# Depthwise convolution of k and v as diagonal products on TensorE, with a re-costed plan, in a hybrid S5 / RWKV-7 layer

## Chip, cores and metric

One core of one Trainium2 chip. The metric is device time of one launch in microseconds (us); less is better.

## What is computed

One layer over 512 latent tokens x (an 8 x 64 grid, 1024 channels) with 256 context tokens in front, all in float32. mod_x and mod_c are nine vectors of 1024 from silu(c) @ w_mod + b_mod.

```python
x   = half_ffn(x, mod_x, 0, ...)
ctx = half_ffn(ctx, mod_c, 0, ...)
hc, hx = modulate(ctx, ...), modulate(x, ...)
_, ctx_states = token_mixers(hc, 1, zero_states, p, False)
out_x, _ = token_mixers(hx, rows, ctx_states, p, True)
x = x + mod_x[5] * out_x
x = half_ffn(x, mod_x, 2, ...)
return rmsnorm(x, final_g)
```

token_mixers projects with w_in into u, r|k|v, three low-rank pieces and two gates; u runs through a bidirectional S5 (a complex recurrence of 64 states in each of 32 groups); r, k and v go through a depthwise 3x3 convolution (`centred_conv`, zero padding; one row of 256 for the context) and then a bidirectional RWKV-7 with 8 heads of 64. Both results are normed, gated, projected and summed.

## The kernel before

**Data.** Activations lie with channels on partitions and tokens along the free axis. A float32 product is made as three fp32r products (`mm3`: hi x hi, lo x hi, hi x lo): each 128 x 1024 weight item is loaded raw by SP, ACT casts it to wh, and POOL or DVE subtracts to give wl (`w_split`, L306, which picks the engine of the subtraction). One item of w_in for the latent tokens is then 24 products of 128 x 512 on PE.

**Order.** The work is written as generators with priorities. A planner (`Plan`, L52) keeps a modelled time for every engine, and at build time runs the generator of best priority whose needs are ready by its model; so it writes one fixed program, and each engine then works through its own rows strictly in order. All DMAs are issued by SP, also in order. A DMA into a buffer that is still read holds up every DMA behind it on SP.

**Stages.** (1) Modulation, then the context's first FFN. (2) The latent tokens' first FFN, with the context's mixers as side streams. (3) b1 (`phase_b1`, `win_items` L1126, `win_mm` L1154): latent projections in the order low-rank pieces, four u items, then k, v, r for each j = 0..3 (a j is 128 channels, two heads); for each a convolution, then `pa`, `pn` and `pb` (L1267 to L1419), which scale k by decays into the RWKV operands (tiles nb, kt, st) and send them to DRAM (abk, lf). `s5_in` (L1690) multiplies u (tiles U, gt), and `s5_rec` (L1723) runs 63 dependent steps of four 128 x 64 operations on POOL (tiles t, hs). `fill_run` (L542) is 16 modulation units of j = 5..8, each two 512 KB loads (wmod, two buffers), eight small products, a row copy (mrow) and two products with sel. (4) b2 (`phase_b2`, L1793): the RWKV chunks (tiles AB, M, Z, Tl), `s5_out` (L1741: tiles hs, gt, U, Tz), `s5_post` (gelu, tiles yi, ga, yg), the glu items, with the 17 gate items of w_in as filler on PE. (5) The output projections. (6) The second FFN of the latent tokens.

**The convolution.** `conv_evac` copies the projection from PSUM into a padded tile (10 x 66, on ACT), makes the centre tap on ACT, and `conv` adds eight taps on DVE, per block of 128 channels:

```python
V.scalar_tensor_tensor(o3, pad[:, dy:dy + 8, dx:dx + 64], cw[:, t:t + 1], o3,
                       op0=OP.mult, op1=OP.add)
```

There are 12 blocks (r, k, v for four j). Two pads alternate, so a block's evacuation waits for the convolution two blocks earlier.

**The products of pb.** Per j and direction d, nb, kt and two of the five st pieces are made on POOL, the other three on DVE:

```python
Pg.tensor_mul(nb, fw(nkk, d), ic)
Pg.tensor_mul(kt, kt, fw(k, d))
Pg.tensor_mul(st[hi, :, 1], nb[hi], em[hi, :, 1:65])
Pg.tensor_mul(st[lo, :, 1], kt[lo], em[lo, :, 1:65])
```

Every instruction is recorded under one line, so the trace is read by the names of tiles.

Of the kernel before, what the change touches and what calls it, by code (L numbers as in the profile page):

```python
# [28 lines left out]
SPD = 0  # L29
# [6 lines left out]
FILLP = 10  # L36
# [7 lines left out]
UAT = 0  # L44
# [7 lines left out]
class Plan:  # L52
# [8 lines left out]
    def __init__(self, nc):  # L61
        self.nc = nc
        self.free = dict.fromkeys("VAPTSHD", 0.0)
        self.w, self.r, self.ev, self.streams = {}, {}, {}, []
        self.tick, self.work, self.cold = 0, 0.0, False
        self.filler, self.quota, self.recent = None, None, []
        for name, e in (("vector", "V"), ("scalar", "A"), ("gpsimd", "P"), ("tensor", "T"), ("sync", "S")):
            setattr(self, name, PlanEngine(self, getattr(nc, name), e))
# [33 lines left out]
    def step(self, e, cost, out, ins, work=0.0):  # L102
# [3 lines left out]
        t = max(t, self.unread(out))  # L106
        if e == "T":
# [4 lines left out]
            self.work += work  # L112
# [75 lines left out]
class PlanEngine:  # L188
# [3 lines left out]
    def __getattr__(self, name):  # L192
        f, plan, e = getattr(self.eng, name), self.plan, self.e

        def g(out, *args, **kw):
# [4 lines left out]
            elif e == "T":  # L200
                k, m = min(i.partition_size() for i in ins), out.partition_size()
                n = out.nbytes() // (4 * m)
                if ins[0].dtype == F32R:
                    c = max(107.0, n / 2.4)
                elif name == "transpose":
                    c = n / 1.2
                else:
                    c = max(n, m) / 1.2 if min(m, k) <= 64 else max(n, 128) / 0.6
                    if m <= 32 and n > 128:
                        c = n / 2.4  # L210
                plan.step(e, c, out, ins, n * k * m / 16384 * (1 if ins[0].dtype == F32R else 2))
            else:
# [6 lines left out]
                elif e == "V" and name == "scalar_tensor_tensor":  # L219
                    a = 130  # L220
                elif e == "V" and name in ("tensor_scalar", "tensor_copy", "memset"):
                    b = 0.52
# [4 lines left out]
                plan.step(e, a + b * n, out, ins)  # L227
# [34 lines left out]
class Kern:  # L262
# [43 lines left out]
    def w_split(self):  # L306
# [16 lines left out]
        eng = nc.vector if (i < self.n_post + 2 or i >= self.n_ffn) and f["P"] - max(f["V"], self.sch.t) > SPD else nc.gpsimd  # L323
# [830 lines left out]
    def win_mm(self, r, m, wh, wl):  # L1154
# [6 lines left out]
        if M_R <= m < M_WD:  # L1161
            n, q = r.n_conv, len(r.names)
            r.n_conv += 1
            yield [f"conv{r.s}{n - 2}"] * (n >= 2) + [f"pb{r.s}{n // q - 2}", f"vr{r.s}{n // q - 2}"] * (n >= 2 * q)
# [3 lines left out]
        else:  # L1168
            self.win_evac(r, m, px)

# [34 lines left out]
    def conv_evac(self, r, n, m, px):  # L1205
# [3 lines left out]
        pad = r.pads[n % 2]  # L1209
        o = r.q.tile([128, r.n], F32, name="cv" + "rkv"[ch // 4], bufs=2)  # L1210
        if r.v:
            A_.copy(pad[:, 1:257], px)
        else:
            A_.copy(pad[:, 1:9, 1:65], px.rearrange("p (y x) -> p y x", x=64))
# [3 lines left out]

    def conv(self, r):
        V = self.nc.vector  # L1220
        for i in range(4 * len(r.names)):
            yield [f"cve{r.s}{i}"]
            n, ch, o = r.cvq[i]
            j, name = ch % 4, "rkv"[ch // 4]
            pad = r.pads[n % 2]
            cw = self.cw[:, ch]
            yield [pad, o, ("V", 500)]
            if r.v:
                for t in (0, 2):
                    V.scalar_tensor_tensor(o, pad[:, t:t + 256], cw[:, 3 + t:4 + t], o, op0=OP.mult, op1=OP.add)  # L1230
            else:
                o3 = o.rearrange("p (y x) -> p y x", x=64)
                for t in (0, 1, 2, 3, 5, 6, 7, 8):
                    dy, dx = divmod(t, 3)
                    V.scalar_tensor_tensor(o3, pad[:, dy:dy + 8, dx:dx + 64], cw[:, t:t + 1], o3,
                                           op0=OP.mult, op1=OP.add)
                    if t in (1, 3, 6):
                        yield [("V", 500)]
            r.cv[name, j] = o
            self.sch.post(f"conv{r.s}{n}")  # L1240
            self.sch.post(f"cv{name}{r.s}{j}")
# [25 lines left out]
    def pa(self, r):  # L1267
# [3 lines left out]
        for j in range(4):  # L1271
# [24 lines left out]
            for i in (2 * j, 2 * j + 1):  # L1296
# [3 lines left out]
                cm = q.tile([128, nch, 65], F32, name="cm")  # L1300
                V.tensor_sub(cm, s65, s65[:, :, 32:33].to_broadcast([128, nch, 65]))
                yield [cm, ("A", 1000)]
                ep = q.tile([128, nch, 65], F32, name="ep", bufs=2)
# [811 lines left out]
```

## Time and profile before

| | us |
|---|---|
| median of 3 runs | 1918.43 (1918.2, 1918.43, 1923.06) |
| the profiled execution | 1924.01, span 1922.3 |
| busy in the span: PE, DVE, ACT, POOL | 1701.1, 917.5, 721.4, 866.6 |
| mean granted clock of TensorE | 0.927 |

The stages, read from the trace, end at about 290 (context FFN), 890 (latent FFN), 1148 (b1), 1411 (b2), 1545 (output projections) and 1922 us (second FFN). The granted clock is a share of the upper of two levels, 2.4 GHz; the lower is 1.2 GHz. An fp32 product is recorded as two instructions.

### The profile page before, as it was taken

Reading aid. Unit: us, or ns where it says so; the run is one execution under the profiler, and the core shown is the slowest. Engines: PE = TensorE matmul, PEld = TensorE weight load, DVE = VectorE, ACT = ScalarE, POOL = GpSimd, SP = SyncE. Lnnn points to the kernel's source line nnn. Section 1 sums busy time; section 2 is a strip of 40 time slices with the busy share of each in tenths; the row PEclk is TensorE's granted clock in tenths of the full one; section 3 lists DMA queues with packets and bytes.
Section 4 is the critical chain, followed back from the end, with each engine's and each line's share of the span. In section 5 each row is a group of like instructions: output and inputs, shape, how many; then the busy total and the mean of one; then the engine's idle time right before and its main releaser. Section 6 shows DMA issues by size and latency. Waiting matters only on the chain.

```text
span 1922.3 us, 33127 instructions
## 1 busy us (share of the span) xinstructions
PE 1701.1 (88%) x13208; PEld 1411.5 (73%) x13208; DVE 917.5 (48%) x1680; ACT 721.4 (38%) x1205; POOL 866.6 (45%) x882
## 2 busy tenths in 40 slices
PE   6999998899999799988887458999987999999996
PEld 3789987677777667877665226777777988888886
DVE  3376454676757364136887616463433331111214
ACT  3355442345453134235554111356443342222221
POOL 1145442456556247432658984101165324444441
PEclk9989999898999899988998558999998999999998
DMA  9865541444554753343553566746364123233331
GB/s 309 299 193 186 189 143 56 123 125 126 148 164 128 199 177 98 91 150 99 164 173 115 158 202 196 217 134 182 128 198 152 56 77 99 89 98 99 101 108 44
DMA packets 235626, 278.43 MB, mean 145 GB/s; under 512 B 93616, under 2 KB 186800, under 8 KB 234448
## 3 DMA queue, kind: packets, MB, share of 16 engines
q1 hardware_dynamic: 235472, 276.32, 47.0%
q8 instruction: 104, 1.70, 0.4%
q14 instruction: 50, 0.41, 0.1%
HBM read 234.31 MB, written 43.22 MB: 144 GB/s over the span
## 4 chain that ended last, share of the span: by engine, by line
PE 55%; DVE 13%; DMA 11%; POOL 8%; ACT 6%; issue 6%; SPq 2%; DVEq 0%; ACTq 0%; POOLq 0%
PE b L196 55%; DMA wmod<-in_wmod 3%; POOL t L196 3%; SPq L196 2%; POOL wl L196 2%; ACT wh L196 2%; DMA AB<-abk 2%; DMA gt<-gates 1%; DVE wl L196 1%; DMA raw<-in_win 1%; DMA raw<-in_wgu 1%; DVE prod L196 1%; POOL hs L196 1%; DVE cvk L196 1%; DVE st L196 1%
## 5 line engine op out<-in xcount | busy, mean ns | idle before, releaser
L196 POOL TENSOR_TENSOR wl<-raw,wh 128x1024 fp32r<-128x1024 f32 x202 | 488.1, 2421 | 842.5 <-ACT wh L196 809.0
L196 PE MATMUL b<-hx,wh 128*128 128x512 f32 (+1 forms) x2432 | 704.4, 377 | 17.2 <-ACT wh L196 11.0
L196 PEld LDWEIGHTS b<-hx,wh 128*128 128x128 f32 x2432 | 441.0, 196 | 93.4 <-ACT wh L196 12.6
L196 PE MATMUL b<-hx,wl 128*128 128x512 f32 (+1 forms) x1216 | 451.2, 371 | 11.3 <-POOL wl L196 11.2
L196 ACT CAST wh<-raw 128x1024 fp32r<-128x1024 f32 x273 | 283.2, 1046 | 226.6 <-DMA raw<-in_wgu 102.7
L196 PEld LDWEIGHTS b<-hx,wl 128*128 128x128 f32 x1216 | 237.6, 195 | 53.4 <-POOL wl L196 14.9
L196 PE MATMUL b<-ah,wh 128*128 128x512 f32 (+1 forms) x560 | 200.4, 358 | 8.7 <-DVE prod L196 3.2
L196 PE MATMUL b<-al,wh 128*128 128x512 f32 (+1 forms) x560 | 196.7, 351 | 0.1
L196 PE MATMUL b<-ah,wl 128*128 128x512 f32 (+1 forms) x560 | 196.5, 351 | 0.1
L196 PE MATMUL b<-hc,wh 128*128 128x256 f32 x928 | 177.0, 292 | 1.2 <-ACT hc L196 1.2
L196 DVE TENSOR_TENSOR prod<-sil,b 128x512 f32<-128x512 f32 (+1 forms) x68 | 39.6, 583 | 262.8 <-PE b L196 245.3
L196 DVE TENSOR_TENSOR wl<-raw,wh 128x1024 fp32r<-128x1024 f32 x71 | 103.8, 1463 | 126.9 <-ACT wh L196 126.0
L196 PEld LDWEIGHTS b<-hc,wh 128*128 128x128 f32 x928 | 149.5, 197 | 10.5 <-issue 7.3
L196 PE MATMUL b<-hc,wl 128*128 128x256 f32 x464 | 133.3, 287 | 0.5 <-POOL wl L196 0.5
L196 PEld LDWEIGHTS b<-ah,wh 128*128 128x128 f32 x560 | 109.2, 195 | 25.3 <-DVE prod L196 3.8
L196 ACT CAST ah<-prod 128x512 fp32r<-128x512 f32 (+1 forms) x68 | 36.6, 538 | 233.6 <-DVE prod L196 233.6
L196 PEld LDWEIGHTS b<-ah,wl 128*128 128x128 f32 x560 | 109.2, 195 | 14.0 <-POOL wl L196 0.6
L196 PEld LDWEIGHTS b<-al,wh 128*128 128x128 f32 x560 | 109.5, 195 | 12.3 <-DVE al L196 0.3
L196 PE MATMUL b<-wmod,zs 128*32 128x256 f32 x576 | 62.5, 534 | 41.8 <-DMA wmod<-in_wmod 41.7
L196 DVE SCALAR_TENSOR_TENSOR x1c<-b,gp,x1c 128x512 f32<-128x512 f32 (+1 forms) x67 | 44.0, 662 | 100.2 <-PE b L196 100.2
L196 PEld LDWEIGHTS b<-hc,wl 128*128 128x128 f32 x464 | 91.2, 197 | 0.7 <-POOL wl L196 0.7
L196 ACT ACTIVATE sil<-b 128x512 f32<-128x512 f32 (+1 forms) x68 | 35.0, 515 | 144.1 <-PE b L196 143.9
(289 smaller groups left out, 2359.3 us busy)
## 6 DMA issues: line engine op xcount, KB each, us to landing
raw<-in_wgu SPq DMA_DIRECT2D x132, 512.0 KB, 3.6
wmod<-in_wmod SPq DMA_DIRECT2D x72, 512.0 KB, 6.0
raw<-in_wdn SPq DMA_DIRECT2D x66, 512.0 KB, 3.8
raw<-in_win SPq DMA_DIRECT2D x49, 512.0 KB, 4.1
gt<-GTd SPq DMA_DIRECT2D x32, 256.0 KB, 3.6
abk<-st SPq DMA_DIRECT2D x8, 1024.0 KB, 5.5
AB<-abk SPq DMA_DIRECT2D x8, 1024.0 KB, 6.3
Hd<-H SPq DMA_DIRECT2D x32, 128.0 KB, 1.9
```

The source lines that it names most:

```text
L196: r = f(out, *args, **kw)
```

## The change

- **Convolution.** For the latent tokens k and v (8 of 12 blocks) go to PE: `taps` (POOL) builds nine diagonal 128 x 128 matrices dg of one block, and `conv_mm` adds nine fp32 products of the unpadded 8 x 64 tile in one PSUM bank, each trimmed by `reach` to the tokens that its tap reaches (1 of 512 columns, 2 of 448, 2 of 504, 4 of 441). ACT copies the sum out. r (4 blocks) stays on DVE, trimmed in the same way. There are three pads.
- **pb.** nb, kt and the two st pieces go from POOL to DVE, for both kinds of token. `pa` does without the tile cm.
- **wl.** The subtraction goes to DVE unless POOL would be done sooner by the model (1150 ns there, 2300 ns on POOL), in the same ranges of items as before.
- **Order.** The u items stand behind k, v, r of j = 3 (UAT 3). The modulation filler has priority 5 and starts with b1. The planner's costs are replaced, and DVE and POOL share a port in its model.

In instructions: PE +72 products; DVE -96 convolution steps of 128 x 512, +32 trimmed steps and 4 scalings, +64 products of pb, wl 71 to 144; POOL wl 202 to 129, -64 products of pb, +8 builds of dg.

```diff
-FILLP = 10
+FILLP = 5
-UAT = 0
+UAT = 3
...
-                self.cold = self.work < 2800
+                self.cold = self.work < 1400
...
-                    c = max(107.0, n / 2.4)
+                    c = max(107.0, n / 2.4) + 13
...
+                port = e == "P" or e == "V" and sum(x.space != PSUM and x.free_size() > 1 for x in ins) > 1
+                plan.step(e, a + b * n, out, ins, port=port)
...
-        eng = nc.vector if (i < self.n_post + 2 or i >= self.n_ffn) and f["P"] - max(f["V"], self.sch.t) > SPD else nc.gpsimd
+        late = max(f["P"], self.sch.t) + 2300 > max(f["V"], self.sch.t) + 1150
+        eng = nc.vector if (i < self.n_post + 2 or i >= self.n_ffn) and late else nc.gpsimd
...
     def fill_run(self, pool):
+        yield ["qx"]
         yield from self.mod_run([(j, u) for j in (5, 6, 7, 8) for u in range(4)], pool, 2, lambda j: 2)
...
+    def taps(self, r, ch):
+        self.dg = r.q.tile([128, 9, 128], F32, name="dg")
+        self.nc.gpsimd.affine_select(self.dg, self.cw[:, ch, :, None].to_broadcast([128, 9, 128]),
+                                     pattern=[[0, 9], [1, 128]], base=0, channel_multiplier=-1,
+                                     compare_op=OP.is_equal, fill=0.0)
...
+    def conv_mm(self, r):
...
+        for i, t in enumerate((4, 0, 1, 2, 3, 5, 6, 7, 8)):
+            o, i_ = self.reach(t)
+            self.nc.tensor.matmul(o3[o], dg[:, t], pad[i_], start=i == 0, stop=i == 8, skip_group_check=True)
+            if i % 2:
+                yield
+        if ch < 11:
+            self.taps(r, ch + 4 if ch < 8 else ch - 3)
+        o = r.q.tile([128, r.n], F32, name="cv" + name, bufs=2)
+        self.nc.scalar.copy(o, px)
...
+            for t in (0, 1, 2, 3, 5, 6, 7, 8):
+                a, b = self.reach(t)
+                V.scalar_tensor_tensor(o3[a], pad[b], cw[:, t:t + 1], o3[a], op0=OP.mult, op1=OP.add)
...
-                Pg.tensor_mul(nb, fw(nkk, d), ic)
-                Pg.tensor_mul(kt, kt, fw(k, d))
+                V.tensor_mul(nb, fw(nkk, d), ic)
...
-                Pg.tensor_mul(st[hi, :, 1], nb[hi], em[hi, :, 1:65])
+                V.tensor_mul(st[hi, :, 1], nb[hi], em[hi, :, 1:65])
...
+                V.tensor_mul(kt, kt, fw(k, d))
```

Three places show how the rows move; (hx, wh or wl) is a projection item, (wmod, zs) a modulation unit.

PE, the end of b1, before: the last product of the last projection item, and what stands behind it.

```order
L196 MATMUL b_10617<-hx_109,wl 128x512
L196 MATMUL b_10519<-wmod,zs 32x256 x4
L196 MATMUL b_10669<-st 32x32 x32
L196 MATMUL b_10717<-sel,mrow 128x2 x2
L196 MATMUL b_10723<-wmod,zs 32x256 x8
L196 MATMUL b_10769<-st 32x32 x32
L196 MATMUL b_10820<-sel,mrow 128x2 x2
L196 MATMUL b_10826<-wmod,zs 32x256 x4
L196 MATMUL b_10854<-blk_1119,sqk 128x2 x4
```

From here to the end of b1 there is no projection item left; PE has the modulation units and the small products of pb.

PE, the end of b1 in the change (the st and ks products of the last pb):

```order
L209 MATMUL b_10802<-hx_109,wh 128x512
L209 MATMUL b_10802<-hx_110,wh 128x512
L209 MATMUL b_10802<-hx_109,wl 128x512
L209 MATMUL b_10851<-st 32x32 x32
L209 MATMUL b_10893<-ks,rkb 128x512
L209 MATMUL b_10946<-hx_109,wh 128x512
```

The last of the four u items (96 products) ends here; they stand among the small products of this last pb. All 13 modulation units of b1 are in its first third, before the convolutions of j = 1, and `s5_in`, which needs all of u, is in b2.

SP, the start of b1, before and then in the change (lt<-tlo and udx<-gst are the low-rank and u transfers):

```order
L196 DMA wmod<-in_wmod 128x4x256 x2
L196 DMA lt_9158<-tlo 64x512
L196 DMA lt_9159<-tlo 64x512
L196 DMA lt_9160<-tlo 64x512
L196 DMA lt_9161<-tlo 64x512
L196 DMA raw<-in_win 128x1024
L196 DMA wmod<-in_wmod 128x4x256
L196 DMA raw<-in_win 128x1024 x3
L196 DMA udx<-gst 128x8x64
```

```order
L209 DMA wmod<-in_wmod 128x4x256 x6
L209 DMA lt_9104<-tlo 64x512
L209 DMA lt_9105<-tlo 64x512
L209 DMA lt_9106<-tlo 64x512
L209 DMA lt_9107<-tlo 64x512
L209 DMA raw<-in_win 128x1024
L209 DMA wmod<-in_wmod 128x4x256 x11
L209 DMA raw<-in_win 128x1024 x2
L209 DMA wmod<-in_wmod 128x4x256 x7
```

Eleven, then seven wmod loads stand in a row, each waiting for one of two buffers, with loads of projection items (raw) behind them.

POOL, the start of the recurrence (copy of s5e), before in b1 and then in the change in b2:

```order
L196 TENSOR_TENSOR nb<-kkr,ic 128x512
L196 TENSOR_TENSOR kt_10088<-kt_10088,cvk 128x512
L196 TENSOR_TENSOR st<-nb,em 64x8x64
L196 COPY hs<-s5e 128x64
L196 TENSOR_TENSOR t_10131<-arr,hs 128x64
L196 TENSOR_TENSOR t_10132<-aii,hs 128x64
L196 TENSOR_TENSOR t_10131<-t_10131,hs 128x64
L196 TENSOR_TENSOR hs<-t_10131,t_10132 128x64
L196 TENSOR_TENSOR st<-kt_10088,em 64x8x64
```

```order
L209 MEMSET tt_10933 32x8x32 x2
L209 AFFINE_SELECT Tl<-ones 128x1024
L209 TENSOR_TENSOR wl<-raw,wh 128x1024
L209 COPY hs<-s5e 128x64
L209 TENSOR_TENSOR t_11377<-arr,hs 128x64
L209 TENSOR_TENSOR t_11378<-aii,hs 128x64
L209 TENSOR_TENSOR t_11377<-t_11377,hs 128x64
L209 TENSOR_TENSOR hs<-t_11377,t_11378 128x64
L209 TENSOR_TENSOR t_11410<-arr,hs 128x64
```

Before, the steps stand between the products of pb; in the change between the set-up of the solves (Tl) and, among the later steps, six more wl subtractions, all in b2.

## Rows read from the trace of the kernel before

**Rows 1.** Stages by window: length, busy of PE, PEld, DVE, ACT, POOL, PEclk, DMA share, GB/s
```profile
290.00:890.00 600.00, 540.96 (x3795) 447.89 (x3793) 326.46 (x644) 236.96 (x420) 292.54 (x352) 0.94 0.45 130
890.00:1053.00 163.00, 137.06 (x1002) 98.43 (x1002) 129.76 (x155) 80.36 (x136) 101.46 (x102) 0.91 0.48 146
1053.00:1148.00 95.00, 46.89 (x503) 23.23 (x499) 44.59 (x68) 16.48 (x33) 86.96 (x187) 0.54 0.59 177
1148.00:1411.00 263.00, 240.58 (x3250) 195.31 (x3251) 134.20 (x263) 118.55 (x205) 68.00 (x73) 0.95 0.57 171
1545.00:1922.00 377.00, 359.10 (x1706) 301.89 (x1704) 88.88 (x162) 100.51 (x137) 150.51 (x70) 0.98 0.29 90
```

**Rows 2.** Chain of waits near the end of b1: start us, us, what
```profile
1117.43 6.36 DMA wmod<-in_wmod
...
1123.83 1.13 PE b L196 x8
...
1137.29 3.54 DMA wmod<-in_wmod
```

**Rows 3.** PE groups in 890 to 1148: count | busy, mean ns | idle before, releaser
```profile
L196 PE MATMUL b<-wmod,zs 128*32 128x256 f32 x208 | 25.7, 586 | 30.4 <-DMA wmod<-in_wmod 30.4
...
L196 PE MATMUL b<-U,gt 128*64 128x64 f32 x256 | 10.6, 232 | 3.2 <-ACT a L196 1.8 <-DMA gt<-GTd 1.2 <-ACT hs L196 0.2
...
L196 PE MATMUL b<-ks,rkb 128*128 128x512 f32 x8 | 6.7, 932 | 5.6 <-DVE ks L196 3.1 <-DVE mod L196 2.5
```

**Rows 4.** Timeline of PE's weight loads: start us, us
```profile
927.72 0.42 PEld L196 LDWEIGHTS b<-vs,flip 128*128 128x128 f32 x2
928.38 0.19 PEld L196 LDWEIGHTS b<-hx,wh 128*128 128x128 f32 x1 [0.24 <-issue]
928.81 0.19 PEld L196 LDWEIGHTS b<-hx,wh 128*128 128x128 f32 x1 [0.24 <-issue]
929.04 0.19 PEld L196 LDWEIGHTS b<-hx,wl 128*128 128x128 f32 x1
```

**Rows 5.** POOL groups in 890 to 1148
```profile
L196 POOL TENSOR_TENSOR wl<-raw,wh 128x1024 fp32r<-128x1024 f32 x11 | 29.5, 2682 | 50.6 <-ACT wh L196 50.6
L196 POOL TENSOR_TENSOR t<-aii,hs 128x64 f32<-128x64 f32 x54 | 26.4, 489 | 0.0
...
L196 POOL TENSOR_TENSOR nb<-kkr,ic 128x512 f32<-128x512 f32 x8 | 12.5, 1564 | 6.5 <-DVE cvv L196 6.5
```

**Rows 6.** DVE groups in 890 to 1148
```profile
L196 DVE SCALAR_TENSOR_TENSOR cvk<-pad,cw,cvk 128x512 f32<-128x512 f32 x32 | 31.1, 973 | 0.8
...
L196 DVE TENSOR_TENSOR st<-kt,em 64x512 f32<-64x512 f32 x8 | 8.2, 1021 | 0.2
```

**Rows 7.** Timeline of POOL: first operation of consecutive recurrence steps at three places
```profile
994.84 0.76 POOL L196 TENSOR_TENSOR t<-arr,hs 128x64 f32<-128x64 f32 x1
...
998.02 0.65 POOL L196 TENSOR_TENSOR t<-arr,hs 128x64 f32<-128x64 f32 x1
...
1127.95 0.32 POOL L196 TENSOR_TENSOR t<-arr,hs 128x64 f32<-128x64 f32 x1
...
1129.29 0.32 POOL L196 TENSOR_TENSOR t<-arr,hs 128x64 f32<-128x64 f32 x1
...
1172.18 0.47 POOL L196 TENSOR_TENSOR t<-arr,hs 128x64 f32<-128x64 f32 x1
...
1174.03 0.37 POOL L196 TENSOR_TENSOR t<-arr,hs 128x64 f32<-128x64 f32 x1
```

**Rows 8.** PE groups in 1148 to 1411: the products of s5_out
```profile
L196 PE MATMUL b<-hs,gt 64*64 64x64 f32 x512 | 20.4, 326 | 0.4 <-issue 0.4
...
L196 PE MATMUL b<-U,Tz 128*64 128x64 f32 x128 | 5.9, 234 | 5.4 <-DMA U<-udx 4.0 <-ACT bt L196 1.5
```

**Rows 9.** Timeline of ACT: first and last piece of s5_post's gelu
```profile
1291.49 1.28 ACT L196 ACT_TABLE_LOAD   x1 [1.86 <-DMA yi<-yd]
...
1316.67 0.62 ACT L196 CAST yg<-ga 128x512 fp32r<-128x512 f32 x1
```

More of the change, by code (lines that the diff above doesn't have):

```diff
@@ L100, in unread, with shared, step @@
         return max([i[4] for i in self.over(self.r, self.box(x))], default=0.0)
-    def step(self, e, cost, out, ins, work=0.0):
+    def shared(self, t, cost):
+        self.port = [i for i in self.port if i[1] > min(self.free["V"], self.free["P"])]
+        for a, b in self.port:
+            if t + cost <= a:
+                break
+            t = max(t, b)
+        self.port = sorted(self.port + [(t, t + cost)])
+        return t
+    def step(self, e, cost, out, ins, work=0.0, port=False):
         t = self.free[e]
@@ L106, in step @@
         t = max(t, self.unread(out))
+        if port:
+            t = self.shared(t, cost)
         if e == "T":
@@ L109, in step @@
                 self.tick += 1
-                self.cold = self.work < 2800
+                self.cold = self.work < 1400
                 self.work = 0.0
-            self.work += work
+            self.work += cost
             self.recent.append((t, work))
@@ L1169, in win_mm @@
             self.win_evac(r, m, px)
+        if not r.v:
+            while len(r.cvq) > (M_K <= m < M_WD):
+                yield from self.conv_mm(r)
     def rot(self, dst, src):
@@ L1208, in conv_evac @@
         ch = m - M_R
-        pad = r.pads[n % 2]
+        pad = r.pads[n % len(r.pads)]
+        if not r.v:
+            A_.copy(pad.rearrange("p y x -> p (y x)"), px)
+            if ch < 4:
+                self.sch.post(f"cve{r.s}{n}")
+            else:
+                r.cvq.append((n, ch))
+            return
         o = r.q.tile([128, r.n], F32, name="cv" + "rkv"[ch // 4], bufs=2)
[L1211 to L1214, printed above, removed]
+        A_.copy(pad[:, 1:257], px)
         A_.activation(o, px, AF.Copy, scale=self.cw[:, ch, 4:5])
@@ L1222, in conv @@
+        for i in range(4 * len(r.names) * r.v):
             yield [f"cve{r.s}{i}"]
             n, ch, o = r.cvq[i]
-            j, name = ch % 4, "rkv"[ch // 4]
-            pad = r.pads[n % 2]
-            cw = self.cw[:, ch]
+            pad, cw = r.pads[n % 2], self.cw[:, ch]
             yield [pad, o, ("V", 500)]
[L1228 to L1238, printed above, removed]
@@ L1452, in phase_b1 @@
         r.lt = [[r.q.tile([128, r.n], F32R, name=f"lt{w}{d}") for d in range(2)] for w in range(2)]
-        r.pads = [T(f"pad{i}", 258) if r.v else T(f"pad{i}", 10, 66) for i in range(2)]
-        for t in r.pads:
-            nc.gpsimd.memset(t, 0.0)
+        r.pads = [T(f"pad{i}", 258) if r.v else T(f"pad{i}", 8, 64) for i in range(3 - r.v)]
+        if r.v:
+            for t in r.pads:
+                nc.gpsimd.memset(t, 0.0)
+        else:
+            self.taps(r, M_K - M_R)
         r.s65 = [T(f"s65{i}", r.nch, 65) for i in range(2)]
```

71 lines of the change are left out of this document (55 added, 16 removed).

## Prediction

> **What bounds the kernel now.** I read the stages first, each by its window [rows 1]. In the second FFN PE is busy 359.10 of 377 us; there the change moves only wl subtractions, which PE does not wait for. The latent FFN with the context's mixers is similar: 540.96 of 600. The hole is in b1. In its first part (890 to 1053) PE is busy 137.06 of 163 and DVE 129.76: two engines hold each other, since a convolution on DVE comes between a projection and the next use of its pad. In its second part (1053 to 1148) PE is busy only 46.89 of 95 and its granted clock is 0.54, about the lower level; POOL is busy 86.96. The last projection item has gone by then, and what is left is pb, the recurrence and modulation. The chain of waits there runs through the modulation loads [rows 2], 6.36 us early and 3.54 us late, each followed by 1.13 us of PE; on PE they cost 30.4 us of idle time in b1 [rows 3]. In b2 PE is busy 240.58 of 263 at a clock of 0.95: RWKV chunks, s5_out and glu with the gate items between them.
>
> So b1 is 258 us in which PE works 184 (137.06 + 46.89), part of it slowly. That is the stage to win, and the change pays with PE time and with a recurrence that starts later.
>
> **b1, step by step.**
> *PE work that stays.* 47 us of the tail ran at 0.54. At the 0.95 of its neighbour stages they would be about 46.89 x 0.54 / 0.95 = 27, so 137 + 27 = 164 us. The small modulation and st products may not scale with the clock, so this is a low estimate by at most 20.
> *s5_in leaves.* 10.6 us [rows 3], so 153.
> *Diagonal products come.* An fp32 product of 512 columns goes in two passes. The loads after the flip product stand 0.43 apart (928.38 to 928.81), those of the fp32r items 0.23 (928.81 to 929.04) [rows 4], so one fp32 product is 0.86 us. A block has 512 + 2 x 448 + 2 x 504 + 4 x 441 = 4180 columns, 8.16 of such products: 7.0 us. Eight blocks: 56 us. Upper bound: the small fp32 group ks, rkb has a busy mean of 932 ns for each of its two records [rows 3], but that is pipelined, partly at the low clock, and not a spacing; by half of it above my value a block would be 8 to 10 us, eight blocks 64 to 80. I take 56, since all are in one full stretch of PE. Sum: 209 us.
> *What leaves the other engines is covered.* DVE loses 64 convolution steps of 0.97 us (62 us) [rows 6] and trims 32 more; it gains nb, kt and two st of each of eight pb, 32 products at no more than the 1.02 us that such a piece took beside POOL [rows 6], 33 us, and some wl. With 174 us before (129.76 + 44.59) it ends at about 140 at most, below PE's 209. POOL loses 32 products of about 1.56 us [rows 5] (50 us) and the 54 steps that it did in b1 (100 us: four operations of 489 ns or a little less), and gains eight dg builds of some 2 us each, as its wl (1024 elements, two inputs, 2.68) bounds them. It is then idle most of the stage. ACT loses a scaling and gains a copy per block. These cost nothing while PE is the bound; if PE were not, DVE would come next.
> *Waits that remain on PE.* The 13 modulation units now stand early, with up to eleven loads in a row on SP and raw loads behind them. At the end of b1 before, 26 loads with two buffers went at about one per 2.5 us (512 KB at the 177 GB/s of that window [rows 1] is 3.0; the pieces of the chain overlap in pairs [rows 2]). So they need 65 to 78 us. PE has in the same rows 96 item products (22 us), two convolution blocks (14), 104 modulation products (14 at the 1.13 of rows 2) and some 20 of low-rank and small products: 70. The loads are thus nearly covered; I take a third to a half of the 30.4, 13 us, with ends of 0 and 51 (13 units at 5.0 us less 1.1 of PE, none covered).
> *Sum for b1:* 209 + 13 = 222 against 258: **-36 us**.
>
> **b2.** s5_in and the recurrence now lie in it, in one chain: s5_in, 63 steps, s5_out, s5_post, glu, the four gate items behind it.
> *s5_in ends* about 42 us into the stage: 98 item products (22), its own 10.6, and 9 of AB products and waits.
> *The recurrence.* A step was 3.18 us beside the convolutions (994.84 to 998.02), 1.34 with DVE quiet (1127.95 to 1129.29), 1.85 beside the solves (1172.18 to 1174.03) [rows 7]. In b2 it lies beside solves, M, Z and some wl on DVE: I take 1.6, between the last two, so 101 us, and six wl of some 2.5 [rows 5] on POOL between: 116. It ends at 158. PE has 215 item products (49 us) and four to five chunks to do meanwhile, so s5_out is about due then.
> *s5_out:* 26.3 us of products [rows 8] and four loads of U and Tz of up to 6 us that no gate item covers any longer: 50, to 208. *s5_post:* gelu from 1291.49 to 1316.67 [rows 9] before, 25 to 27, to 235. *glu and four gate items:* 144 products at 0.23, 33, and some 11 of chunk products and waits between: to 279. Before, b2 was 263: **+16 us**, between 0 (the RWKV chunks end last, as before) and 100 (rival below).
>
> **Other stages.** In the context's part pb's products go to DVE too; DVE is busy 326.46 of 600, so there is room, and PE's idle 59 us shrink or grow a little: -5, between -25 and +12.
>
> **Sum:** -36 + 16 - 5 = **-25 us**. The profiled execution took 1924.0, 5.6 above the median of the three runs, so it would become 1899 and the median **1893**. A measurement of this kernel tells about 0.3% (5.8 us) from no change.
>
> **The Trainium skill on the recurrence.** By the Trainium skill, SBUF - State Buffer, section "Who interferes with whom", a DVE instruction with two SBUF inputs and a GpSimd one that reads SBUF exclude each other, and a DVE instruction with one SBUF input does not disturb GpSimd. By that rule only the solves, Z and wl would delay the steps and M, which reads PSUM, would not, so the first rival below would not come. The trace agrees as far as it goes: 3.18 beside back-to-back convolution steps, 1.34 beside none.
>
> **Rivals.**
> 1. *The recurrence crawls* (slower). If DVE's wl and M make a step 3.18 us as beside the convolutions, 63 steps and six wl take 215, the recurrence ends at 257 instead of 158, nothing is left to fill PE, and b2 is 99 longer: 1992. It cancels the gain from 2.0 us per step (25 / 63 more than 1.6). For it: some wl now on DVE in that stretch. Against it: the 1.85 beside the solves, which are also full DVE work. Chance 0.07.
> 2. *The modulation loads stall the in-order PE and SP* (slower). No cover: 51 us of waits instead of 13, so 1931; it cancels the gain at 25 us beyond my 13. For it: eleven loads in a row with raw loads behind them on SP. Against it: 70 us of other products in the same rows. Chance 0.10.
> 3. *More gain.* The waits are near 0, and the chunks still end b2, so nothing is added there: 1893 - 13 - 14 = 1866. For it: PE has less idle time in the stages that are planned full. Chance 0.20.
> 4. *The gain is eaten in the middle.* The change does not shorten b1 by what it removes, because the tail was never DVE's: diagonal products at 9 us (+16) with +12 in the context stage give 1921, no change. Chance 0.09.
>
> **How the numbers follow.** My forecast's own range is 1875 to 1911, with 0.54. With rival 3 it is faster: 0.74. No change 0.09, slower 0.17. The range to hold eight in ten: from 1862 (rival 3 and a little more) to 1933 (rival 2).
>
> **What would show it.** In the trace after: b1 some 36 us shorter with the clock in its last 95 us at 0.9 or more; each dg product at 0.8 to 0.9 us start to start; modulation waits on PE below 20 us; the first and the last recurrence step in b2, 1.4 to 1.8 us apart; s5_out 160 us into b2. If b1 is as long as before, the dg products or the loads were mis-sized; if b2 is over 300, the recurrence was; if the gain comes from the FFN stages, the whole sum looked at the wrong place.

## Result and the profile after

The changed kernel takes 1967.22 us (median; 1963.54 to 1970.4) against 1918.32 in the same comparison: a ratio of 1.0244 [1.0219, 1.027]. I had forecast 1893 and a range up to 1933. It is 49 us slower where I had said 25 faster. The profiled execution took 1963.54, its span is 1961.8. It is the shortest of four, and the one profiled before (1924.01) lay above its median; so the two spans differ by 39.5 us where the medians differ by 49.

I cut the stages at events of the program, since their times move: b1 begins with the first low-rank product of the latent tokens and ends with the last ks,rkb product (or the last modulation product, where that is later); b2 ends with the first output projection. The marks are read to about 2 us. By these marks b1 runs from 895 to 1148 before and b2 to 1411, and the columns of the windows are those of [rows 1]. First the kernel before, by these marks:

```profile
290.00:895.00 605.00, 544.60 (x3803) 450.33 (x3802) 329.00 (x645) 238.00 (x420) 294.89 (x353) 0.93 0.45 130
895.00:1148.00 253.00, 180.31 (x1495) 119.22 (x1493) 171.81 (x221) 95.80 (x167) 186.07 (x287) 0.78 0.52 159
```

The changed kernel: the context stage (with the latent tokens' first FFN), b1, b2 and the second FFN.

```profile
290.00:936.00 646.00, 555.61 (x3819) 459.14 (x3818) 348.10 (x690) 236.79 (x416) 236.04 (x307) 0.89 0.42 122
936.00:1149.00 213.00, 201.55 (x1383) 125.62 (x1383) 124.83 (x204) 87.59 (x132) 32.00 (x38) 0.97 0.53 160
1149.00:1456.00 307.00, 251.25 (x3499) 204.46 (x3500) 136.58 (x261) 120.85 (x230) 122.31 (x283) 0.91 0.57 166
...
1585.00:1961.80 376.80, 360.04 (x1707) 303.24 (x1705) 133.54 (x200) 100.24 (x137) 60.46 (x32) 0.98 0.28 90
```

Read it downward against before. b1 is 40 us shorter, with PE busy 201.55 of 213 at a clock of 0.97: the hole is gone, as forecast. The context stage is 41 longer (605 to 646), though PE is busy only 11 more there, with nearly the same number of products (3819 for 3803) at a clock of 0.89 for 0.93. b2 is 44 longer (263 to 307), though PE works only 10.7 more than in [rows 1]. So PE lost its time by waiting, in two places, and not by the new products. The second FFN is unchanged, and the output projections take 129 instead of 134. Together 41 - 40 + 44 - 5 = 40, the difference of the two spans.

**The context stage.** PE's waits in 290 to 936 (total us, times, longest):

```profile
PE b L209 <- POOL X L209: 22.4, 13, 4.0
PE b L209 <- DVE cb L209: 13.3, 9, 2.1
PE b L209 <- DVE cvv L209: 13.1, 2, 11.6
```

All three belong to the context's mixers: X and cb are tiles of their S5 set-up, cvv is their convolution of v. Where they sit the timeline of PE shows (start, us, what, the wait before it): from 431 to 497 ten groups of four products with the identity, with cb behind each group, and no product of the FFN between them.

```profile
434.84 0.35 PE L209 MATMUL b<-ident,X 128*128 128x128 f32 x1 [3.19 <-POOL X L209]
...
437.26 0.90 PE L209 MATMUL b<-ident,X 128*128 128x128 f32 x3 [2.08 <-POOL X L209]
437.96 1.75 PE L209 MATMUL b<-cb,X 128*128 128x32 f32 x8
...
443.67 0.47 PE L209 MATMUL b<-ident,X 128*128 128x128 f32 x1 [3.96 <-POOL X L209]
```

This stretch and the wait for cvv behind it account for the loss. Here is 431 to 511 in the changed kernel, and then in the kernel before:

```profile
431.00:511.00 80.00, 34.25 (x161) 26.55 (x159) 58.58 (x128) 10.87 (x26) 46.61 (x65) 0.55 0.38 103
431.00:511.00 80.00, 75.71 (x469) 63.04 (x468) 50.15 (x89) 40.18 (x68) 50.40 (x52) 0.91 0.50 141
```

PE is idle 46 us of 80 where it was idle 4, and its granted clock there is 0.55, near the lower level. The timeline of DVE at 504 shows why cvv is late. In the S5 set-up's loop an H waits for its transfer Hd, in 13 of 16 turns; here a turn takes 3.6 us, 1.13 of them this wait, and everything behind the loop on DVE waits too: nb, which the change put there, and behind that cvv, for which PE stands 11.6 us.

```profile
507.84 0.42 DVE L209 TENSOR_TENSOR H<-mh 128x256 f32<-128x256 f32 x1 [1.13 <-DMA Hd<-H]
509.43 0.42 DVE L209 TENSOR_TENSOR nb<-kkr,ic 128x256 f32<-128x256 f32 x1
510.10 1.00 DVE L209 SCALAR_TENSOR_TENSOR cvv<-pad,cw,cvv 128x256 f32<-128x256 f32 x2
```

**b2.** Two waits make up most of PE's 56 us of idle time there:

```profile
PE b L209 <- DMA T<-ti: 19.2, 4, 13.8
PE b L209 <- ACT yg L209: 15.7, 4, 9.4
```

T is the end of the solves, yg that of s5_post. Both depend on POOL, whose timeline shows the recurrence: its first step, in the middle of which it waited 16.52 for hs; Tl, which belongs to the solves and stands between its steps; and a stretch in its middle.

```profile
1198.53 0.32 POOL L209 TENSOR_TENSOR t<-t,hs 128x64 f32<-128x64 f32 x1 [16.52 <-ACT hs L209]
...
1212.79 2.05 POOL L209 TENSOR_SCALAR_AFFINE_SELECT Tl<-ones 128x1024 f32<-128x1024 f32 x1 [9.84 <-DMA ti<-Tl]
...
1239.22 0.32 POOL L209 TENSOR_TENSOR t<-arr,hs 128x64 f32<-128x64 f32 x1
1240.57 0.32 POOL L209 TENSOR_TENSOR t<-arr,hs 128x64 f32<-128x64 f32 x1
...
1242.25 0.47 POOL L209 TENSOR_TENSOR t<-aii,hs 128x64 f32<-128x64 f32 x1
1242.69 0.48 POOL L209 TENSOR_TENSOR t<-t,hs 128x64 f32<-128x64 f32 x1
...
1249.82 2.36 POOL L209 TENSOR_TENSOR wl<-raw,wh 128x1024 fp32r<-128x1024 f32 x1 [6.20 <-ACT wh L209]
```

Undisturbed steps are 1.35 us apart (1239.22 to 1240.57). A wl among them takes not its 2.36 alone but 6.20 of waiting before it, for ACT's cast wh. The recurrence ends at 1347, 198 us into b2; s5_out follows to 1396.5, yg comes at 1405.8, the first output projection at 1456.

### The profile page after: what moved, and what is told of

Same layout as the page of the kernel before. It is cut to its first block, busy times and chain, and to the rows that moved or that the text cites. A ratio compares the mean times of both kernels' runs of the same rounds, so it can differ in the third digit from the quotient of the medians.

```text
span 1961.8 us, 33397 instructions
## 1 busy us (share of the span) xinstructions
PE 1737.7 (89%) x13352; PEld 1430.2 (73%) x13352; DVE 951.3 (48%) x1757; ACT 714.6 (36%) x1194; POOL 599.4 (31%) x751
## 4 chain that ended last, share of the span: by engine, by line
PE 62%; DMA 14%; DVE 9%; ACT 5%; issue 5%; POOL 3%; SPq 2%; DVEq 0%; ACTq 0%; POOLq 0%
PE b L209 62%; DMA wmod<-in_wmod 2%; SPq L209 2%; ACT wh L209 2%; DMA raw<-in_wgu 2%; POOL wl L209 1%; DVE wl L209 1%; DMA gt<-gates 1%; DMA gt<-GTd 1%; DMA Hd<-H 1%; DMA ti<-AT 1%; DMA U<-udx 1%; DMA raw<-in_win 1%; DVE st L209 1%; DMA Z<-vt 1%
## 5 line engine op out<-in xcount | busy, mean ns | idle before, releaser
L209 POOL TENSOR_TENSOR wl<-raw,wh 128x1024 fp32r<-128x1024 f32 x129 | 312.9, 2429 | 919.6 <-ACT wh L209 875.8
L209 DVE TENSOR_TENSOR wl<-raw,wh 128x1024 fp32r<-128x1024 f32 x144 | 192.3, 1336 | 300.5 <-ACT wh L209 298.1
L209 PEld LDWEIGHTS b<-hx,wl 128*128 128x128 f32 x1216 | 237.1, 195 | 49.0 <-POOL wl L209 10.7
L209 PE MATMUL b<-wmod,zs 128*32 128x256 f32 x576 | 53.5, 461 | 21.9 <-DMA wmod<-in_wmod 21.5
```

The lines of the kernel that those rows point to most:

```text
L209: r = f(out, *args, **kw)
```

## Experiments

The runs by stage (us; start of b1, lengths of b1 and b2 from each run's trace; the ratio is to the kernel before on the same chip). Each edit is planned anew, so the order of rows away from the edit can move with it. The theory's times came true in norec and cp_gatewl; ctxpool gained more than its theory said; in the others the rival held, or neither did:

| run | b1 begins | b1 | b2 | median | ratio [95%] |
|---|---|---|---|---|---|
| before | 895 | 253 | 263 | 1918.32 | 1 |
| after | 936 | 213 | 307 | 1967.22 | 1.0244 [1.0219, 1.027] |
| ctxpool | 887 | 213 | 310 | 1915.36 | 0.9977 [0.9952, 1.0002] |
| oldwl | 932 | 219 | 309 | 1968.66 | 1.0242 [1.0207, 1.0278] |
| convonly | 893 | 291 | 265 | 1949.98 | 1.0162 [1.0125, 1.02] |
| noconv | 885 | 225 | 297 | 1918.5 | 0.9991 [0.9972, 1.001] |
| nca_u3 | 881 | 237 | 296 | 1923.49 | 1.0001 [0.9979, 1.0024] |
| nca_u1 | 888 | 264 | 271 | 1940.92 | 1.0098 [1.0061, 1.0135] |
| nca_u0 | 884 | 276 | 283 | 1964.29 | 1.02 [1.0168, 1.0233] |
| uat0 | 941 | 271 | 270 | 1995.28 | 1.0391 [1.0333, 1.0448] |
| gatewl | 939 | 216 | 303 | 1962.92 | 1.0208 [1.017, 1.0246] |
| norec | 943 | 218 | 284 | 1939.46 | 1.0095 [1.0063, 1.0126] |
| ctxpool_glup0 | 891 | 213 | 305 | 1922.76 | 1.0008 [0.9988, 1.0027] |
| cp_g0_u2 | 895 | 255 | 269 | 1949.48 | 1.0149 [1.011, 1.0187] |
| dverec_all | 885 | 218 | 323 | 1945.02 | 1.0132 [1.0106, 1.0157] |
| dverec_16 | 885 | 215 | 309 | 1925.68 | 1.0025 [1.0008, 1.0041] |
| dverec_noconv | 891 | 239 | 320 | 1961.26 | 1.0213 [1.0183, 1.0243] |
| cp_gatewl | 883 | 216 | 303 | 1913.45 | 0.9943 [0.9922, 0.9965] |
| cp_gatewl_prio | 878 | 219 | 306 | 1916.37 | 0.9969 [0.9944, 0.9995] |

### Who lost the context stage?

Theory: pb's products of the context on DVE, whose queue the S5 set-up holds. Rival: the new rule that spreads wl over DVE and POOL.

**ctxpool** gives the context's products back to POOL; the latent tokens' stay on DVE.

```
+        Pb = Pg if r.v else V
-                V.tensor_mul(nb, fw(nkk, d), ic)
+                Pb.tensor_mul(nb, fw(nkk, d), ic)
...
-                V.tensor_mul(kt, kt, fw(k, d))
+                Pb.tensor_mul(kt, kt, fw(k, d))
```

> The change, with nb, kt and two st products of pb back on POOL for the context tokens alone (latent tokens keep them on DVE). Theory (the 40 us lost before b1 come from a crowded DVE in the context's part: subtractions and pb there push back the context's convolution, the projections behind it wait, and PE runs the S5 set-up without FFN products from 431 to 511): the bare stretch goes, b1 begins 25 to 40 us earlier (896 to 911 instead of 936), the kernel takes 1930 to 1942 us instead of 1967. Rival (the new costs in the planner make a worse order whoever does the products): b1 still begins after 925, the kernel stays above 1955.

b1 begins 49 us earlier, at 887, and the ratio falls from 1.0244 to 0.9977 [0.9952, 1.0002]: the whole loss. PE's waits in 290 to 887 of this kernel:

```profile
PE b L209 <- DVE cb L209: 7.5, 3, 3.2
PE b L209 <- POOL X L209: 5.9, 3, 3.3
```

The wait for cvv is no longer among the largest, and that for X fell from 22.4 to 5.9, although the edit does not touch X. PE is no longer left alone with the set-up: its longest stretch without a product of the FFN or of a projection is 65 us in the change (431 to 497), 26.5 here (428 to 454.5) and 10 in the kernel before. The order is the planner's; why it comes out so with the products on DVE is not shown. The waits for Hd by themselves are not the loss: DVE is idle for them 41.5 us in the kernel before, 21.8 in the change and 37.6 here. What counts is what stands behind them, and what PE has to do meanwhile.

**oldwl** restores the old rule for wl.

```
-        late = max(f["P"], self.sch.t) + 2300 > max(f["V"], self.sch.t) + 1150
-        eng = nc.vector if (...) and late else nc.gpsimd
+        eng = nc.vector if (...) and f["P"] - max(f["V"], self.sch.t) > SPD else nc.gpsimd
```

> The change, with the rule of before for the engine of the wl subtraction (DVE only where the model has POOL free later than DVE). Theory: in the context's part DVE is relieved of some 15 subtractions of 1.3 us and b1 begins 20 to 40 us earlier (896 to 916); in b2 more subtractions stand on POOL between the recurrence steps, each held up by the cast that PE's pace sets, so the recurrence takes as long as or longer than the 147 us of the change and b2 stays at 300 to 320: 1930 to 1950 us. Rival (planner's costs): b1 begins after 925, above 1955. A third possibility, that the subtractions on DVE were also what delayed the solves in b2, would show as b2 under 290.

No gain: 1.0242 [1.0207, 1.0278]. PE's waits in 290 to 932 and DVE's timeline where the largest ends:

```profile
PE b L209 <- DVE st L209: 49.3, 2, 47.5
```

```profile
617.40 0.42 DVE L209 TENSOR_TENSOR H<-mh 128x256 f32<-128x256 f32 x1 [1.14 <-DMA Hd<-H]
619.00 0.42 DVE L209 TENSOR_TENSOR st<-kk,ep 128x256 f32<-128x256 f32 x1
619.33 0.87 DVE L209 TENSOR_TENSOR st<-nb,em 64x256 f32<-64x256 f32 x2
```

The loss has another face. Here nb runs at 572, ahead of the H loop; the pieces of st stand behind it (st<-kk,ep was on DVE before, too; one of the next two was moved there), and PE waits 47.5 us in one piece. The rule for wl is not the cause; the products on DVE are: b1 begins at 932 to 943 in all five kernels that have the context's products there (after, oldwl, uat0, gatewl, norec), and at 878 to 895 in the other fourteen.

### What are the diagonal products worth?

**convonly** is the kernel before with the change's convolution alone: k and v on PE, r trimmed, pa without cm.

```
+            while len(r.cvq) > (M_K <= m < M_WD):
+                yield from self.conv_mm(r)
...
+        for i, t in enumerate((4, 0, 1, 2, 3, 5, 6, 7, 8)):
+            o, i_ = self.reach(t)
+            self.nc.tensor.matmul(o3[o], dg[:, t], pad[i_], start=i == 0, stop=i == 8, skip_group_check=True)
```

> The kernel before with one part of the change alone: the convolution of k and v as diagonal products on TensorE (with the tile cm left out of pa, to have the room). Modulation late, u early, pb's products on POOL, the planner's costs and the rule for wl as before. Theory (b1 became 40 us shorter because the diagonal products and the new order go together: the products relieve DVE, while the u items and the early modulation fill PE's bare tail): with the products alone PE has 56 us more to do and the bare tail with its modulation loads stays, so b1 takes 240 to 275 us (258 before), the kernel 1905 to 1940. Rival (taking the convolution from DVE is by itself the gain): b1 takes 210 to 230, the kernel 1875 to 1895.

By themselves they cost 1.0162 [1.0125, 1.02]. b1 is 291 long, beyond the 275 of the theory: PE is busy 241.61 of it, 61 more than before, at a clock of 0.81. DVE is busy 52 us less (119.80 for 171.81), which does not shorten it, and PE still waits 18.3 us for modulation loads.

**noconv** is ctxpool with the convolution back on DVE.

```
-        if not r.v:
-            while len(r.cvq) > (M_K <= m < M_WD):
-                yield from self.conv_mm(r)
...
+                    V.scalar_tensor_tensor(o3, pad[:, dy:dy + 8, dx:dx + 64], cw[:, t:t + 1], o3,
```

> The change with the context's pb products on POOL (the run of that name took 1915), and the convolution of the latent k and v back on DVE as before; u last, modulation early, planner and wl as in the change. Theory: DVE then holds b1 with 64 more steps of some 0.7 to 1.0 us, b1 takes 235 to 265 us instead of 213 and the kernel 1935 to 1970. Rival (the order alone made b1 shorter): b1 stays at 205 to 225, the kernel at 1905 to 1925. A diagonal product block should show 7.0 us of PE in the run that has it, so b1 here would be shorter than 213 if only PE bounded it.

0.9991 [0.9972, 1.001], no different from ctxpool. Here are its b1 and b2, and then those of ctxpool:

```profile
885.00:1110.00 225.00, 170.40 (x1342) 115.09 (x1342) 170.29 (x259) 92.33 (x147) 34.57 (x36) 0.83 0.53 163
1110.00:1407.00 297.00, 249.57 (x3398) 205.37 (x3395) 133.63 (x263) 117.56 (x219) 123.33 (x281) 0.88 0.55 162
```

```profile
887.00:1100.00 213.00, 201.32 (x1383) 125.87 (x1381) 122.73 (x204) 87.69 (x132) 32.17 (x38) 0.97 0.53 161
1100.00:1410.00 310.00, 253.71 (x3495) 206.12 (x3496) 135.21 (x263) 121.32 (x230) 120.13 (x281) 0.89 0.55 163
```

The diagonal products shorten b1 by 12 us, not by the 48 that they take from DVE (170.29 to 122.73), and b2 gives 13 back. The rest of b1's gain, 253 to 225, is there without them (nca_u3 below splits it).

### What made b2 longer?

Theory: the recurrence, now in b2, holds s5_out and with it glu. Rivals: u's late place as such, POOL's wl between the steps, glu's priority.

**norec** runs one of the latent tokens' 63 recurrence steps; 62 are left out.

```
-        for c in range(1, 32 if r.v else 64):
+        for c in range(1, 32 if r.v else 2):
```

> The change with one step of the latent recurrence instead of 63 (62 steps of four POOL operations are left out, so the S5 part of the output is another one). Theory (of the 44 us by which b2 grew, 11 are the S5 input products and the other 33 come from the recurrence being late: S5 output and glu stand behind spent filler): without the steps S5 output and glu run among the gate items, b2 takes 265 to 280 us instead of 307 and the kernel 1925 to 1945. Rival (the solves and chunks, slowed by the subtractions on DVE, end b2 whatever the recurrence does, as the run with the subtractions on DVE suggests, where the recurrence was shorter and b2 not): b2 stays at 295 or more, the kernel at 1955 to 1970.

The ratio falls from 1.0244 to 1.0095 [1.0063, 1.0126], some 28 us. Its b2, and PE's largest wait there:

```profile
1161.00:1445.00 284.00, 254.39 (x3495) 203.68 (x3496) 131.88 (x263) 123.91 (x232) 28.11 (x31) 0.93 0.60 176
```

```profile
PE b L209 <- DMA AB<-abk: 13.0, 4, 5.7
```

b2 is 23 shorter. The waits for T (19.2) shrink to 0.7 and those for yg (15.7) are gone; 13.0 for AB take part of their place. So the recurrence does lengthen b2, by both chains that pass through POOL. How much of the 44 it accounts for is less sure: this trace is of the longest of ten executions, 1957.86 with a median of 1939.46, so b2 may be shorter than 284 in the others.

**gatewl** gives the wl of all gate items to DVE, so that none stands between the steps.

```
-and late else
+and (late or self.n_gate <= i < self.n_post) else
```

> The change, with all subtractions of the 17 gate items on DVE, so that POOL has nothing but the solve set-up between the recurrence steps in b2. Theory: the recurrence takes 95 to 110 us instead of 147, S5 output products begin 15 to 35 us earlier, b2 shrinks from 307 to 275 to 292: 1935 to 1952 us. Rival (the chunks and solves on DVE end b2, and more subtractions on DVE delay them): the recurrence is as short, but b2 stays above 300 and the kernel at 1960 to 1980.

The recurrence shrinks from 148 us to 114 (1204 to 1318), yet b2 is only 4 shorter and the ratio is 1.0208 [1.017, 1.0246], not told apart from the change's. The longest wait of PE in b2 is still for T:

```profile
PE b L209 <- DMA T<-ti: 21.7, 4, 15.3
```

```profile
1319.65 0.28 PE L209 MATMUL b<-T,M 32*32 32x32 f32 x2 [15.30 <-DMA T<-ti]
```

This wait ends behind the recurrence, and the s5_out products on hs, which stand among the chunks in PE's order, begin at 1335 and end at 1397, where they ended in the change's own run. An earlier recurrence alone gains nothing that can be told.

**uat0** lets u begin behind the first head block again. That is its place in the kernel before: the low-rank pieces, k, v, r of j = 0, then the four u items, and not u ahead of all k, v, r.

```
-UAT = 3
+UAT = 0
```

> The change, with the u items back behind j = 0, so that u, the S5 input products and the recurrence lie in b1 again. Theory (b2 became 44 us longer because the recurrence waits there on in-order POOL behind subtractions): b1 grows by 10.6 us of S5 input products and 5 to 15 us of bare tail, b2 comes back to 260 to 275, sum 1935 to 1955. Rival (b2 is longer because the solves and chunks are slower or the filler is spent, whatever the recurrence does): b2 stays above 290 and the kernel is at 1975 to 1990. The start of b1 stays at 936 by both.

b2 is back at 270, but b1 is 271, and the whole is 1.0391 [1.0333, 1.0448]. PE's waits around b1:

```profile
PE b L209 <- DVE ks L209: 16.4, 1, 16.4
PE b L209 <- DVE st L209: 14.6, 4, 8.2
PE b L209 <- ACT kt L209: 11.1, 1, 11.1
```

With u's items gone early, PE has nothing to do at the end of b1 while pb goes through DVE and ACT. Beside it, u behind k, v, r takes 58 us from b1 and puts 37 into b2.

**ctxpool_glup0** and **cp_g0_u2** change glu's priority in ctxpool, and then u's place by one.

```
-GLUP = 4
+GLUP = 0
...
-UAT = 3
+UAT = 2
```

> The change with the context's pb products on POOL, and the four gate items that stand behind the glu items moved ahead of them (GLUP 0), so that they fill PE while it waits in b2 for the recurrence and for the solves. Theory (b2 is 47 us longer because its PE filler is spent by two fifths of the stage, PE then waits on the chain recurrence, S5 output, gelu, glu, and the four items stand behind that chain): the 22 us of the four items go into holes, b2 shrinks from 310 to 285 to 295, the kernel takes 1890 to 1902 us instead of 1915. Rival (the items only delay the chunks and the S5 output products by as much): 1910 to 1920.

> As the run before it, and the u items behind k, v, r of j = 2 instead of j = 3 (UAT 2), so that the S5 input products lie in the last part of b1 and the recurrence begins some 40 us earlier, with the items of j = 3 still to come for PE. Theory: b1 grows by 10.6 us of products and 5 to 20 of bare tail (213 to 230 to 245), b2 has its filler and its chain again side by side and takes 260 to 275: 1880 to 1905 us. Rival (the recurrence on POOL slows pb on DVE at the end of b1, as where u stood behind j = 0 and b1 took 272): b1 above 255 and the kernel above 1915.

glu's priority does nothing that can be told (1.0008 [0.9988, 1.0027] against 0.9977 [0.9952, 1.0002]). One place earlier for u gives a b2 of 269 and a b1 of 255, and costs 1.4% (1.0149 against 1.0008).

**nca_u3**, **nca_u1**, **nca_u0** have the change's order, planner and wl rule, with the convolution on DVE and pb's products on POOL, as before; u begins behind head block 3, 1 or 0. Against noconv:

```
-        Pb = Pg if r.v else V
+        Pb = Pg
-UAT = 3
+UAT = 1
```

> The order of the change alone: u items last, modulation early, the planner's costs and the wl rule of the change, but the convolution on DVE and pb's products on POOL for both kinds of token as before. Theory (b1 became shorter through the order, which gives PE work for its bare tail, and not through the diagonal products; with pb on POOL, idle in b1, DVE has 33 us less than in the run with the convolution on DVE, where b1 took 226): b1 takes 205 to 225 us, b2 stays at 295 to 310, the kernel at 1895 to 1915. Rival (the diagonal products are needed for the shorter b1): b1 235 to 260, the kernel above 1925.

> As the run before it with the u items behind j = 1 (UAT 1), so that the recurrence begins in b1. Theory: b1 grows by 10.6 us of S5 input products and some contention to 225 to 245, b2 has its chain beside the filler again and takes 265 to 285: 1885 to 1910 us. Rival (recurrence and pb on POOL hold each other up at the end of b1, as before the change): b1 above 250 and the kernel above 1920.

> As the run before it with the u items first (UAT 0): against the kernel before, only the early modulation, the planner's costs and the wl rule are new. Theory: the 30 us that PE waited for modulation at the end of b1 go, POOL with the recurrence and pb then ends b1 at 230 to 250 us, b2 takes 260 to 275: 1890 to 1910 us. Rival (POOL's tail of recurrence and pb alone set the end of b1 before): b1 stays at 253 to 262, the kernel at 1915 to 1925.

The order alone, with the planner's costs and the wl rule, is worth nothing that can be told (1.0001 [0.9979, 1.0024]): b1 is 16 shorter than before and b2 33 longer, while the other stages gain. With it an early u is worse (1.0098, 1.02). By one trace of each, b1's gain of 40 splits so: 253 to 237 by the order, 237 to 225 by the latent tokens' products on DVE (noconv), 225 to 213 by the diagonal products (ctxpool).

### Can the recurrence be made short?

**dverec_all** puts the latent recurrence of ctxpool on DVE in one piece, **dverec_16** in pieces of 16 steps with s5_out's priority at 1, **dverec_noconv** in one piece into noconv.

```
-                sch.add(self.s5_in(X), 3)
-                sch.add(self.s5_rec(X), 2)
+                sch.add(self.s5_in(X), 0)
+                sch.add(self.s5_rec(X), 0)
-        Pg, h = self.nc.gpsimd, r.hs
+        Pg, h = self.nc.gpsimd if r.v else self.nc.vector, r.hs
-            yield [("P", RECP)]
+            if r.v or c % 64 == 0:
+                yield [("P", RECP) if r.v else ("V", 300)]
```

> The change with the context's pb products on POOL, and the 63 recurrence steps of the latent tokens on DVE in one run, with the S5 input products and the recurrence at best priority; nothing is left out. It starts where the recurrence of the change starts, after all u items, and differs in its length and in what stands between its steps. Theory (the recurrence's length on in-order POOL behind subtractions is what costs b2): 252 small operations of 0.2 to 0.27 us are 50 to 68 us instead of 147, S5 output runs among gate items, b2 takes 270 to 290 us instead of 310 and the kernel 1880 to 1897 instead of 1915. Rival (its late start is enough, or the steps on DVE push the solves and chunks back by as much as they gain): b2 at 300 or more, the kernel at 1905 to 1925.

> As the run before, with the recurrence in four pieces of sixteen steps between the solves' operations, and S5 output at priority 1 instead of 2. Theory: the recurrence takes 80 to 110 us, solves and chunks are held up less, b2 takes 275 to 295: 1885 to 1900 us. Rival: b2 at 300 or more, 1905 to 1925.

> The recurrence on DVE in one run with the convolution on DVE as before (the run with that and the recurrence on POOL took 1918; context's pb products on POOL, order and costs of the change). Theory: b1 stays at 226 (13 us above the one with diagonal products), b2 shrinks to 260 to 285 from 297: 1880 to 1900 us. Rival (DVE, which is full to the end of b1 there, delays recurrence and solves): 1905 to 1925. Beside the first run of the three it gives the worth of the diagonal products where the recurrence no longer hides it: 5 to 15 us by theory.

The recurrence fell from 148 us in ctxpool to 57 (70 in pieces), and b2 did not: 323, 309 and 320. In dverec_all PE has one long wait in b2:

```profile
PE b L209 <- DVE hs L209: 43.4, 1, 43.4
```

DVE's solves stand behind the steps: the last T,M products come at 1378 to 1389, in ctxpool at 1311. Two chains need the in-order engines, recurrence to s5_out to glu and solves to chunks to projection, and whichever goes first makes the other late.

### A version that beats both

**cp_gatewl** joins the edits of ctxpool and gatewl. **cp_gatewl_prio** also plans the recurrence first.

```
-                sch.add(self.s5_in(X), 3)
-                sch.add(self.s5_rec(X), 2)
+                sch.add(self.s5_in(X), 0)
+                sch.add(self.s5_rec(X), 0)
-            yield [("P", RECP)]
+            yield [("P", RECP) if r.v else ("P", 300)]
```

> Two edits of earlier runs together: the context's pb products on POOL, and all subtractions of the 17 gate items on DVE. Theory (the two losses are apart: the first edit brought 52 us against the change, the second 4): 1908 to 1914 us, b2 at 300 to 310. Rival (they share a cause): 1914 to 1922.

> As the run before, with the S5 input products and the recurrence at best priority in the plan (0 instead of 3 and 2), so that the recurrence stays on POOL, with no subtractions between its steps, and begins as early as u allows. Theory (by now: b2 holds two chains, recurrence with S5 output and solves with chunks, on one in-order PE; the recurrence alone costs POOL, so that only its own chain moves): S5 output begins 10 to 20 us earlier than in the run before, b2 takes 285 to 300 us, the kernel 1895 to 1908. Rival (what S5 output gains the chunks lose, as with the steps on DVE): within 5 us of the run before.

cp_gatewl takes 1913.45 us, 0.9943 [0.9922, 0.9965]: faster than the kernel before by about half a per cent, and than the change by 2.9% by the two ratios. Its interval overlaps that of ctxpool, so what gatewl adds there isn't settled. The priority adds nothing.

## Why the prediction was wrong, by its own steps

- **b1, "-36 us": right, at -40.** PE became the bound (201.55 of 213) and its clock rose to 0.97. A dg product goes in two passes 0.43 us apart (loads at 976.42 and 976.85), and the block at 1057.57 takes 7.17 us against my 7.0. The modulation waits were 6.0, not 13. The groups of PE in 927 to 1149:

```profile
L209 PE MATMUL b<-pad,dg 128*128 128x441 f32 x64 | 30.2, 554 | 0.0
...
L209 PE MATMUL b<-wmod,zs 128*32 128x256 f32 x220 | 18.1, 408 | 6.0 <-DMA wmod<-in_wmod 6.0
```

- **Who earned it** was not in my sum: I counted PE's work in a full stage. By nca_u3, noconv and ctxpool the order gave 16 of the 40, pb's products 12, the diagonal products 12.
- **"DVE is busy 326.46 of 600, so there is room": the step that failed**, -5 with bounds of -25 and +12, where it was +41. It is an average over 600 us, and the engine works in order: within it the H loop takes 3.6 us or more a turn and waits for a transfer in 13 of 16. I did not list, as I should have, what is queued behind H where the 32 context products were to go, nor what PE has to do meanwhile: from 431 to 511 it is idle 46 us of 80, where it was idle 4. Putting the products back regains 51 us by the two ratios (2.67% of 1918). Of the 65 us between my -25 and the +40 of the two traces, 46 are here and 28 in b2; b1 and the output projections take 9 off.
- **b2, "+16 us, between 0 and 100": right in kind, wrong in size; it was +44.** The step price held (1.48 on average, forecast 1.6), and rival 1 with 3.18 did not come. The sum fails at these terms: s5_in ends 50 us into b2, not 42 (+8). "Six wl of some 2.5" took 7.5 to 8.6 each, but for the last with 3.5, their waits included: 43, not 15 (+28). Tl with the wait before it is 12 and was not in the sum. The 63 steps took the remaining 93 of the 148, not 101 (-8). s5_out took 50, as forecast, s5_post cost PE 9 instead of 27 (-18), and glu with the gate items 50 instead of 44 (+6). 279 + 8 + 28 + 12 - 8 - 18 + 6 = 307, which is b2. This follows one of the two chains; the waits for T (19.2) lie within these terms. norec then gives back 28 us of the whole kernel.
- **The rivals.** "The modulation loads stall" did not come (6.0). "More gain" did in b1 only. "The gain is eaten in the middle" had one right place, the context stage, with +12 as its bound; its other half, diagonal products at 9 us, did not come (7.17). No rival had the context stage as a loss by itself. Two of their sums slipped, without weight here: rival 3 takes back 14 where b2 had added 16 (1864, not 1866), and rival 4 adds its +12 to a sum that held -5 already (1926, not 1921).
- **What I had not seen at all** is that b1 and b2 trade. Their sum is 516 before, 520 after, 523 in ctxpool, 522 in noconv, 519 in cp_gatewl and 524 in cp_g0_u2, while PE's busy time in it goes from 421 (before) and 420 (noconv) to 455 (ctxpool). It is no constant: other orders make it longer, 533 to 559 in the nca runs, 541 in uat0, 556 in convonly, 559 in dverec_noconv. But no kernel with the whole recurrence is below 516; only norec is, at 502. So in these two stages PE's busy time alone does not set the end, and my sum, which moved PE's work and kept the rest, could not hold. Where b2's last ten us come from (284 in norec's long execution, against 263 before and 11 of s5_in) stays open, and so does whether an order of PE exists in which T and the recurrence don't hold each other: only a planner's priorities were tried, not a written order.

On the price of a step two rows of DVE stand against those of POOL above. Beside M the step at 1240.57 runs undisturbed, with operations of 0.32; from 1241.59 the solves run on DVE, and POOL's operations take 0.47 and 0.48 (1242.25, 1242.69).

```profile
1240.38 1.29 DVE L209 TENSOR_TENSOR M<-b,mask 128x512 f32<-128x512 f32 x2 [2.78 <-PE b L209]
1241.59 0.53 DVE L209 TENSOR_TENSOR prod<-Tl,AT 128x231 f32<-128x231 f32 x1
```

By the Trainium skill, SBUF – State Buffer, section "Who interferes with whom", a GpSimd instruction that reads SBUF contends with DVE instructions that have two SBUF inputs, and not with those that have at most one, outside the two-port modes. The trace agrees here: M takes b from PSUM, prod both inputs from SBUF. Beside the step of 3.18 us in [rows 7] DVE ran a wl too (996.54 in the kernel before), not convolution steps alone; that, too, has two SBUF inputs. The loss lay elsewhere, in waits that the price of an instruction does not hold.

## What to carry to other kernels

Before work is moved to an engine with idle time, list what stands in front of it in that engine's order at its new place, and what that waits for; the engine's share of busy time over the stage says nothing of it. When a serial chain is moved to another stage, price what interleaves with it on its engine by the wait before each foreign instruction and not by its length. And if several variants shift time between two neighbouring stages and their sum does not fall, look for the chain that spans both before saving more work on the busiest engine.

## What was unexpected of the hardware

The same recurrence step takes 0.79 us on DVE and 1.35 on POOL, back to back. In dverec_all:

```profile
1147.68 0.22 DVE L209 TENSOR_TENSOR t<-arr,hs 128x64 f32<-128x64 f32 x1
...
1148.47 0.23 DVE L209 TENSOR_TENSOR t<-arr,hs 128x64 f32<-128x64 f32 x1
```

One operation of 128x64 takes 0.22 us there, against 0.32 on POOL [rows 7], a smaller gap than that between the steps. A dg build took 1.41 us where I had estimated 2:

```profile
L209 POOL TENSOR_SCALAR_AFFINE_SELECT dg<-cw 128x1152 f32<-128x1152 f32 x7 | 9.9, 1414 | 85.3 <-PE b L209 64.7 <-DVE cvr L209 20.6
```
